# Two gate blocks as a seventeenth pair, k rows written once in a third buffer, and the first output projection ordered by hand

## The chip, the cores and the metric

The kernel runs on one core of a Trainium2 chip. What is measured is device time in microseconds (us), the median of the timed runs. One more execution is recorded by the hardware profiler; every duration of a single instruction comes from that one. The engines are PE (matrix products), DVE (VectorE), ACT (ScalarE), POOL (GpSimd) and SP, which here only issues DMA transfers, all of them in one queue.

## The reference

One encoder block for a sequence of 1024 rows of width 1024, one layer, all in float32. Cut to what the kernel's stages correspond to:

```python
h = rmsnorm(x, norm_w) * (1 + scale) + shift           # scale, shift, gate from c @ w_ada
(a_bg, a_cg, a_x, a_z, q, k, v, z_b, a_raw, b_raw,
 gate_a_raw, gate_b_raw) = split(h @ w_in)
ya = a_cg * dwconv_centred(a_bg * a_x, conv_a_w)        # width 3
ya = (ya * silu(a_z)) @ w_pa
q, k, v = silu(dwconv_centred([q, k, v], conv_qkv_w))   # width 5, 8 heads of 128
q, k = l2norm(q), l2norm(k)
...
for n in chunks:                                        # gated delta rule, forwards and backwards
    v_new = u[n] - w[n] @ S
    o[n] = q_dec[n] @ S + a_qk[n] @ v_new
    S = S * gl[n] + k_dec[n].T @ v_new
...
o = rmsnorm_per_head(o_forward + o_backward) * gdn_norm_w
yb = (o * silu(z_b)) @ w_pb
merged = sigmoid(gate_a_raw) * ya + sigmoid(gate_b_raw) * yb
out = rmsnorm(x + gate * (merged @ w_o), final_norm_w)
```

u and w come from a triangular inverse for each chunk of each head.

## The kernel before

**Blocks.** The sequence lies along the free dimension, and the 1024 features of h are eight tiles of 128 partitions, each split into two parts, hhi and hlo, whose sum is the float32 value. A column block of w_in is 128 outputs wide. Its product is 3 x 8 x 2 = 48 matmuls of 128x512: high weights by hhi, high weights by hlo, low weights by hhi, for eight tiles and two halves of the sequence. A weight block (`wtile`, line 1123) is two DMAs of 256 KB from SP's queue, a rounding copy on ACT (wh) and a subtraction on POOL (wl) for each half. The gate blocks are named ga0 to ga7 (for the first mixer) and gb0 to gb7, their results pass through a sigmoid and are stored to sga_d and sgb_d.

**Heads.** For each head h one column block each of k, q, v and z is computed. Then `prep_k` (line 770) transposes kT to get row norms (ktp), builds the decay matrices D and the gram product, and inverts 32x32 blocks: 30 pairs of steps (et, E) on POOL, with DMAs through memory before and behind. `prep_q` (851) forms q times the decays (the row of decays er is loaded by DMA, 861), transposes kT once more for the rows of k (ktk, copied to ktok, 883) and v for vp. `merge` (906) joins the 32x32 blocks into 128x128 with small matmuls (psy, psu, pst, psz, psv), with copies on DVE and ACT between. `chain` (983) runs eight steps of state product (cb from S and kT), solve (cb from r and N), scaled copy (vw) and update (cb from vw and ktok), both directions at once. Its output lies in vp, is normalized there, and `head_out` (1065) transposes it (otp), multiplies by silu(z) and stores it to yb_d.

These routines are generators. A scheduler records what they yield (line 294) and issues PE's instructions in an order of its own (line 203), from a table of costs; once issued the order is fixed. `fill` (1078) feeds it the column blocks between: k, q, v and z of the heads, and gate blocks, with three (RESERVE, line 26) held to the end; `choose` (1093 to 1097) picks the next. The pair PLAIN = (2, 6) (line 27) says that gb0 and gb1 are among them, that gb2 to gb5 are run as plain blocks behind the heads, and gb6 and gb7 behind the pairs.

**Pairs.** The 32 column blocks of the first mixer (bg, ax, cg, az) run as 16 pairs (`Pair`, 1189): two column blocks by two halves of the sequence and of the features, with seven products of 12 matmuls instead of eight, 84 matmuls a pair. The operands are sums of weights (DVE), a rounding copy (ACT) and a subtraction (POOL); `slots` (1180) gives them places, four in the weight buffers hi and lo and two in buffers of their own. Weights are prepared five products ahead (AHEAD). `mixed` (1279) consumes the results; behind the az pair of blocks j and j+1 the two y are stored to y_d. The first pair and the last one ("last", 1329) have products in an order of their own.

**Gate blocks and first output projection.** Behind the pairs come gb6 and gb7 (`gate_block`, 1332). The eight tiles of y are loaded from y_d and split into yhi and ylo before gb7 (1364 to 1378). Then the projection by w_pa (1392 to 1416): for each block pa0 to pa7 the weights, the gate sga, the weights wadag of the third part of w_ada, 48 matmuls, a product with the gate, the store to m_d, eight small DVE operations that make ga from wadag, `gate_column` (1388) for the block before, and the split of one tile blo of yb. The pool bs has two buffers for sga and one for wadag, and the order of the engines other than PE is the program scheduler's here, while it is written by hand (`manual_schedule`) in the pairs. Behind it come the projection by w_pb (pb) and the last one by w_o (fo).

## Time and profile before

| what | us |
|---|---|
| median of 3 runs (lowest, highest) | 1502.65 (1497.63, 1503.92) |
| the profiled execution, whole | 1494.86 |
| its span, first to last instruction | 1493.1 |

The mean granted clock of PE in that execution is 0.978 of full speed. By stage of the profiled execution, in us from its start, with the time in which PE was busy:

| stage | from, to | PE busy | granted clock |
|---|---|---|---|
| conditioning, norm, first k | 0, 128 | 102.0 of 128 | 0.84 |
| heads, with gate blocks between | 128, 813 | 653.4 of 685 | 0.99 |
| plain gate blocks gb2 to gb5 | 813, 859 | 46.0 of 46 | 0.98 |
| 16 pairs | 859, 1174 | 310.7 of 315 | 1.00 |
| gb6, gb7, first projection (pa) | 1174, 1307 | 118.1 of 133 | 0.95 |
| second projection (pb) | 1307, 1397 | 90.0 of 90 | 1.00 |
| last projection (fo) | 1397, 1493 | 89.6 of 96 | 0.99 |

A row of such a table counts time in which PE had any instruction, so a PE that runs its instructions at a lower clock, or with a start that waits for each, still reads as busy. In rows of single instructions the columns are the start, the duration, the engine, the line of the kernel, and in brackets how long the engine had been idle before it and what it waited for.

### The profile page before, as it was taken

The numbers are of one execution on the slowest core, as the hardware profiler recorded it, in microseconds if no ns is written. First come the engines' busy times: TensorE is split into PE (matmuls) and PEld (weight loads), VectorE is DVE, ScalarE is ACT, GpSimd is POOL, SyncE is SP. The second block draws the span as 40 slices with busy tenths as digits, with TensorE's granted clock in tenths as the row PEclk, the third lists the DMA queues.
The fourth block names the chain that finished last, engine by engine and source line by source line (L and its number), as shares of the span: only waits on it lengthen the run. The fifth ranks groups of instructions, "written<-read, shape, count | busy, mean of one in ns | idle before, by whom it ended". The sixth has DMA issues, their size and how long they took to land.

```text
span 1493.1 us, 22782 instructions
## 1 busy us (share of the span) xinstructions
PE 1409.8 (94%) x8602; PEld 1168.1 (78%) x8602; DVE 843.4 (56%) x1457; ACT 621.2 (42%) x1498; POOL 690.4 (46%) x861
## 2 busy tenths in 40 slices
PE   4899999999999999999997999999999969999998
PEld 3687878787878787878886878787878758888886
DVE  7959227557666667566524736565657364423335
ACT  5227728657574737474533333222232251122211
POOL 6103649553668448654712654544545122255301
PEclk7799999999999999999999999999999989999999
DMA  8213341412423231513221220303030465455502
GB/s 322 93 40 124 98 125 72 114 50 69 118 63 100 58 113 29 142 30 86 69 60 57 99 99 29 113 29 113 29 106 22 158 255 197 156 191 173 193 14 99
DMA packets 123581, 153.37 MB, mean 103 GB/s; under 512 B 74704, under 2 KB 75088, under 8 KB 123472
## 3 DMA queue, kind: packets, MB, share of 16 engines
q1 hardware_dynamic: 123184, 151.14, 31.6%
q8 instruction: 67, 1.10, 0.3%
q10 hardware_dynamic: 288, 0.79, 0.1%
q14 instruction: 42, 0.34, 0.1%
HBM read 122.40 MB, written 29.49 MB: 102 GB/s over the span
## 4 chain that ended last, share of the span: by engine, by line
PE 66%; DVE 12%; POOL 7%; ACT 6%; DMA 5%; issue 4%; SPq 1%; POOLq 0%; ACTq 0%; DVEq 0%
PE pp_ga L203 6%; PE cb L203 4%; PE pp_q L203 4%; PE ps_ax_S L1233 3%; PE pp_k L203 3%; PE ps_bg_S L1233 3%; PE ps_cg_S L1233 3%; PE pp_z L203 3%; PE ps_az_S L1233 2%; POOL E L294 2%; PE o L203 2%; POOL et L294 2%; PE pp_pb L1138 2%; PE pp_pb L1140 2%; PE pp_pb L1139 2%
## 5 line engine op out<-in xcount | busy, mean ns | idle before, releaser
L294 POOL TENSOR_TENSOR E<-E,et 128x30 f32<-128x30 f32 (+7 forms) x240 | 122.3, 509 | 17.3
L294 POOL TENSOR_TENSOR et<-E 128x30 f32<-128x30 f32 (+7 forms) x240 | 113.1, 471 | 26.1 <-DMA E<-s 9.9
L294 ACT ACTIVATE vw<-cb,cols 128x128 f32<-128x128 f32 x112 | 35.8, 365 | 104.0 <-PE cb L203 103.9
L294 ACT ACT_TABLE_LOAD x49 | 62.9, 1283 | 1.5 <-PEq L1570 0.8
L294 DVE SCALAR_TENSOR_TENSOR S<-S,exps,cb 128x128 f32<-128x128 f32 x96 | 29.1, 342 | 60.8 <-PE cb L203 60.7
L1138 PE MATMUL pp_pa<-yhi,wh_pa 128*128 128x512 f32 x128 | 52.3, 408 | 6.9 <-ACT yhi L1375 6.9
L1130 POOL TENSOR_TENSOR wl_pa<-wr_pa,wh_pa 128x512 fp32r<-128x512 f32 x16 | 24.1, 1523 | 72.3 <-ACT wh_pa L1129 72.3
L1140 PE MATMUL pp_pa<-yhi,wl_pa 128*128 128x512 f32 x128 | 51.7, 404 | 3.0 <-POOL wl_pa L1130 3.0
L203 PE MATMUL pp_ga<-hhi,wh_ga 128*128 128x512 f32 x128 | 51.7, 404 | 1.9 <-ACT xpad L294 1.9
L1139 PE MATMUL pp_pa<-ylo,wh_pa 128*128 128x512 f32 x128 | 51.8, 405 | 1.6 <-DVE ylo L1376 1.6
L203 PE MATMUL pp_ga<-hhi,wl_ga 128*128 128x512 f32 x128 | 52.2, 407 | 0.0
L203 PE MATMUL pp_ga<-hlo,wh_ga 128*128 128x512 f32 x128 | 51.7, 404 | 0.0
L203 PE MATMUL pp_z<-hhi,wl_z 128*128 128x512 f32 x128 | 51.4, 401 | 0.0
L203 PE MATMUL pp_z<-hlo,wh_z 128*128 128x512 f32 x128 | 51.2, 400 | 0.0
L203 PE MATMUL pp_z<-hhi,wh_z 128*128 128x512 f32 x128 | 51.1, 399 | 0.0
L1138 PE MATMUL pp_pb<-bhi,wh_pb 128*128 128x512 f32 x128 | 50.6, 395 | 0.0
L1140 PE MATMUL pp_pb<-bhi,wl_pb 128*128 128x512 f32 x128 | 50.5, 395 | 0.0
L1139 PE MATMUL pp_pb<-blo,wh_pb 128*128 128x512 f32 x128 | 50.5, 395 | 0.0
L294 DVE SCALAR_TENSOR_TENSOR kT<-xpad,cvq_t,kT 128x1024 f32<-128x1024 f32 x32 | 47.7, 1490 | 0.3
L294 POOL TENSOR_TENSOR wl_q<-wr_q,wh_q 128x512 fp32r<-128x512 f32 x16 | 20.8, 1304 | 58.2 <-ACT wh_q L294 54.7
L294 DVE SCALAR_TENSOR_TENSOR qT<-xpad,cvq_t,qT 128x1024 f32<-128x1024 f32 x32 | 47.3, 1480 | 0.4
L294 DVE SCALAR_TENSOR_TENSOR N<-gram,cols,D 128x128 f32<-128x128 f32 x128 | 34.6, 342 | 22.1 <-PE gram L203 16.9
(764 smaller groups left out, 4654.4 us busy)
## 6 DMA issues: line engine op xcount, KB each, us to landing
wada<-in_wada SPq DMA_DIRECT2D x16, 512.0 KB, 7.5
D<-gr_d SPq DMA_DIRECT2D x16, 512.0 KB, 7.8
xt<-in_x SPq DMA_DIRECT2D x8, 512.0 KB, 8.9
wr_k<-in_win SPq DMA_DIRECT2D x16, 256.0 KB, 3.1
wr_q<-in_win SPq DMA_DIRECT2D x16, 256.0 KB, 3.2
wr_v<-in_win SPq DMA_DIRECT2D x16, 256.0 KB, 4.3
wr_ga<-in_win SPq DMA_DIRECT2D x16, 256.0 KB, 3.1
qg<-er_d SPq DMA_DIRECT2D x8, 512.0 KB, 6.2
```

The costliest lines, as they stand in the source:

```text
L203: getattr(self.pe, what)(out, *ins, **kw)
L294: self._sched.record(self._name, lambda: real(*args, **kw), outs, ins, cost, extra, table, op == "memset")
L1130: G.tensor_tensor(lo[:, ch(q, 512)], raw, hi[:, ch(q, 512)].bitcast(F32), ALU.subtract)
L1138: PE.matmul(ps, wh, mhi[k][:, sl], start=i == 0, stop=False)
L1139: PE.matmul(ps, wh, mlo[k][:, sl], start=False, stop=False)
L1140: PE.matmul(ps, wl, mhi[k][:, sl], start=False, stop=i == KT - 1)
L1233: PE.matmul(ps, w[:, ch(m)], r, start=first and m == i == 0, stop=m == 3 and i == 2, skip_group_check=True)
```

## The change

**k rows.** `prep_k` now writes ktok from the transposes ktp that it makes anyway, in three buffers instead of two. The second transposition ktk in `prep_q` goes. One of the two rows of decays is loaded into the buffer vp of the head instead of a buffer of its own (er); so vp is taken earlier, and the wait for the output of head h - 2, whose buffer it is, stands ahead of the load.

**Gate blocks.** PLAIN is (0, 4): the heads' fill has ga0 to ga7 alone, the plain blocks behind the heads are gb0 to gb3. gb4 and gb5 become a seventeenth pair (`stored`), which now is the "last" one. gb6 and gb7 stay behind the pairs. `slots` starts at another place of its six, so that the last product of 17 pairs falls on the same one.

**Before the first projection.** At the fourth-last product of the pairs the program takes the buffers of y, both weight blocks gb6 and gb7, and issues the loads of y. Three tiles of y are split ahead of gb6, five ahead of gb7, and pa0's weights stand between.

**The first projection.** Its order is by hand now. sga, wadag and blo of block j + 1 are fetched at the start of block j, wadag has two buffers, and `gate_column(j)` stands behind block j, no longer one later.

Where instructions stand now is shown at three places. The first is PE's queue at the end of head 6's chain. The names are: o6 the output of the chain, pp_z6 and pp_z7 the column blocks z of heads 6 and 7, psy7 and psu7 the small products that join head 7's inverse, otp6 the transposes of head 6's output. Before:

```order
L203 MATMUL pp_z6_1_7607<-hhi6_574,wl_z6_7275 128x512
L203 MATMUL pp_z6_1_7607<-hhi7_621,wh_z6_7274 128x512
L203 MATMUL pp_z6_1_7607<-hlo7_622,wh_z6_7274 128x512
L203 MATMUL pp_z6_1_7607<-hhi7_621,wl_z6_7275 128x512
L203 MATMUL otp6_0_7670<-ident_72,vp6_6803 128x128 x4
L203 MATMUL otp6_1_7678<-ident_72,vp6_6803 128x128 x4
L203 MATMUL pp_z7_0_7685<-hhi0_101,wh_z7_7556 128x512
```

And after the change, where the row o6 is the last product of the chain:

```order
L204 MATMUL o6_0_7084<-vn6_1_7_7484,D1_6_5679 128x128
L204 MATMUL pp_z6_1_7412<-hlo5_534,wh_z6_6934 128x512
L204 MATMUL pp_z6_1_7412<-hlo7_622,wh_z6_6934 128x512
L204 MATMUL pp_z6_1_7412<-hhi7_621,wl_z6_6935 128x512
L204 MATMUL psy7_7550<-T64_7_7082,N0_7_6479 32x32
L204 MATMUL psy7_7550<-y64_7_7083,N0_7_6479 32x32
...
L204 MATMUL psy7_7550<-y64_7_7083,N1_7_6480 32x32
L204 MATMUL otp6_0_7589<-ident_72,vp6_6506 128x128 x4
L204 MATMUL otp6_1_7595<-ident_72,vp6_6506 128x128 x2
L204 MATMUL psu7_7599<-N0_7_6479,Vb7_7008 32x32 x2
L204 MATMUL psu7_7599<-N1_7_6480,Vb7_7008 32x32 x2
```

Before, the last product of chain 6 stood 69 rows ahead of otp6, and most rows between were column products of v7 and z6, with z7 behind otp6. Now the last eight products of z6 and the 32 small products psy7 stand between them, and the rest of the joining (psu7) comes among the transposes.

The second place is PE's queue at the end of head 7, the last one (o7 the output of its chain, otp7 its transposes, gb and ga7 column blocks). Before:

```order
L203 MATMUL o7_0_7974<-vn7_1_7_8256,D1_7_6598 128x128
L203 MATMUL pp_gb1_1_8203<-hlo6_575,wh_gb1_7942 128x512
L203 MATMUL pp_gb1_1_8203<-hhi6_574,wl_gb1_7943 128x512
L203 MATMUL pp_gb1_1_8203<-hhi7_621,wh_gb1_7942 128x512
L203 MATMUL pp_gb1_1_8203<-hlo7_622,wh_gb1_7942 128x512
L203 MATMUL pp_gb1_1_8203<-hhi7_621,wl_gb1_7943 128x512
L203 MATMUL otp7_0_8297<-ident_72,vp7_7560 128x128 x4
L203 MATMUL otp7_1_8302<-ident_72,vp7_7560 128x128 x4
L1138 MATMUL pp_gb2_0_8391<-hhi0_101,wh_gb2_8355 128x512
```

After:

```order
L204 MATMUL o7_1_7710<-vn7_0_7_8001,D0_7_6477 128x128
L204 MATMUL o7_0_7709<-vn7_1_7_8002,D1_7_6478 128x128
L204 MATMUL pp_ga7_0_7996<-hhi2_103,wh_ga7_7814 128x512
L204 MATMUL pp_ga7_0_7996<-hlo2_107,wh_ga7_7814 128x512
...
L204 MATMUL pp_ga7_1_8042<-hlo7_622,wh_ga7_7814 128x512
L204 MATMUL pp_ga7_1_8042<-hhi7_621,wl_ga7_7815 128x512
L204 MATMUL otp7_0_8083<-ident_72,vp7_7011 128x128 x4
L204 MATMUL otp7_1_8088<-ident_72,vp7_7011 128x128 x4
L1134 MATMUL pp_gb0_0_8177<-hhi0_101,wh_gb0_8141 128x512
```

Five column products of gb1 stood between the last o7 and otp7; now 42 of ga7 stand there, and the first plain block behind is gb0 instead of gb2.

The third place is the queue of SP around the last stores of y (a6, a7) and the loads behind them (wr_ raw weights, ylo the loads of y, sgb_d and sga the gates' stores and loads). Before:

```order
L1316 DMA y_d_87<-a6_10724 128x1024
L1128 DMA wr_gb7_0_11027<-in_win 128x512
L1128 DMA wr_gb7_1_11031<-in_win 128x512
L1370 DMA ylo0_11017<-y_d_87 128x1024
...
L1370 DMA ylo7_11024<-y_d_87 128x1024
L1400 DMA wadag1_11292<-in_wadag 128x1024
L1337 DMA sgb_d_88<-xpad0_116 128x1024
L1128 DMA wr_pa0_0_11098<-in_wpa 128x512
L1128 DMA wr_pa0_1_11102<-in_wpa 128x512
L1398 DMA blo0_11190<-yb_d_89 128x1024
```

After:

```order
L1312 DMA y_d_87<-a6_10510 128x1024
L1124 DMA wr_gb6_0_10893<-in_win 128x512
L1124 DMA wr_gb6_1_10897<-in_win 128x512
L1124 DMA wr_gb7_0_10903<-in_win 128x512
L1124 DMA wr_gb7_1_10907<-in_win 128x512
L1381 DMA ylo0_10883<-y_d_87 128x1024
...
L1381 DMA ylo7_10890<-y_d_87 128x1024
L1337 DMA sgb_d_88<-gb5_10935 128x1024
L1413 DMA sga0_11134<-sga_d_86 128x1024
L1351 DMA sgb_d_88<-xpad0_116 128x1024
L1124 DMA wr_pa0_0_11034<-in_wpa 128x512
L1124 DMA wr_pa0_1_11038<-in_wpa 128x512
L1416 DMA blo0_11120<-yb_d_89 128x1024
```

The weights of both blocks gb6 and gb7 now stand ahead of the loads of y, the weights pa0 behind the gates' stores as before, and one blo stands behind them where all eight stood.

The diff, with unchanged lines left out:

```diff
@@ -24,7 +24,8 @@
 RESERVE = 3
-PLAIN = (2, 6)
+PLAIN = (0, 4)
+LAST = 6
 AHEAD = 5
@@ -772,6 +773,7 @@
         kT = tiles["k", h]
+        ktok = yield big("ktok", f"ktok{h}", 3)
         kss = yield tile_of(gp, [P, 5, NC], "kss", f"kss{h}", 3)
@@ -786,6 +788,7 @@
                 yield tr(ps[:, ch(cc)], kT[:, ch(4 * half + cc)])
+            S.activation(ktok[:, ch(half, 512)], ps, AF.Copy)
             for cc in range(4):
@@ -844,7 +847,7 @@
         Q.dma_start(Vb, s2[1].rearrange("c b r k -> (b r) c k"))
-        ghead[h] = dict(kT=kT, A=D, D=D, N=N, N3=N3, Vb=Vb, bk=bk, wk=wk, sk=kss[:, 3])
+        ghead[h] = dict(kT=kT, ktok=ktok, A=D, D=D, N=N, N3=N3, Vb=Vb, bk=bk, wk=wk, sk=kss[:, 3])
         yield ("mark", ("pk", h))
@@ -858,7 +861,10 @@
         qg = [(yield big("qg0", f"qg0_{h}", 2)), qT]
-        er = [qg[0], (yield big("er", f"er{h}", 1))]
+        if h >= 2:
+            yield ("need", ("out", h - 2))
+        vp = gh["vp"] = yield big("vp", f"vp{h}", 2)
+        er = [qg[0], vp]
         for d in range(2):
@@ -880,18 +886,8 @@
             V.tensor_tensor(qg[d], qT, er[d], ALU.mult)
-        ktok = yield big("ktok", f"ktok{h}", 2)
-        for half in range(2):
-            ps = yield get(pg, f"ktk{h}_{half}", kT)
-            for cc in range(4):
-                yield tr(ps[:, ch(cc)], kT[:, ch(4 * half + cc)])
-            S.activation(ktok[:, ch(half, 512)], ps, AF.Copy)
-            yield free(ps)
-        gh.update(qg=qg, qss=qss, ktok=ktok)
+        gh.update(qg=qg, qss=qss)
         yield ("need", ("v", h))
-        if h >= 2:
-            yield ("need", ("out", h - 2))
-        vp = gh["vp"] = yield big("vp", f"vp{h}", 2)
         vT, sk = tiles["v", h], gh["sk"]
@@ -1175,14 +1171,14 @@
-    place, spare = [2], []
+    place, spare = [-7 * (17 + (LAST - PLAIN[1] - 2) // 2) % 6], []
...
             return [bw.tile([P, 512], F32R, tag=p, name=f"w{p}{name}", bufs=2) for p in "hl"]
-        if i % 2 == 0:
+        if i % 2 == 0 or not spare:
             spare[:] = [wp.tile([P, KT * P], F32R, tag=f"w{p}", name=f"w{p}{name}") for p in ("hi", "lo")]
@@ -1325,8 +1321,26 @@
+    def stored(name, j0, dst, func, place):
+        parts = {}
+
+        def consume(b, half, ps, add):
+            if b not in parts:
+                parts[b] = [bt.tile([P, T], F32, tag="out", name=f"{name}{j0 + b}", bufs=4), 0]
+            o = parts[b][0][:, ch(half, 512)]
+            if add is not None:
+                V.tensor_tensor(o, ps, add, ALU.add)
+                ps = o
+            S.activation(o, ps, func)
+            parts[b][1] += 1
+            if parts[b][1] == 2:
+                Q.dma_start(dst[j0 + b], parts[b][0])
+
+        return Pair(name, j0, consume, place)
+
     pairs = [(n, j) for j in range(0, 8, 2) for n in ("bg", "ax", "cg", "az")]
-    pairs = [mixed(n, j, {0: "first", len(pairs) - 1: "last"}.get(i)) for i, (n, j) in enumerate(pairs)]
+    pairs = [mixed(n, j, None if i else "first") for i, (n, j) in enumerate(pairs)]
+    pairs += [stored("gb", j, sgb_d, AF.Sigmoid, "last" if j + 2 == LAST else None) for j in range(PLAIN[1], LAST, 2)]
     steps = [(p, n) for p in pairs for n in p.order]
@@ -1360,21 +1374,23 @@
             yp = ctx.enter_context(tc.tile_pool(name="yp", bufs=1, reuse_waits="tile", side="right"))
-            ws = [wtile(win[G_B + PLAIN[1]], f"gb{PLAIN[1]}")]
-    yhi = [yp.tile([P, T], F32R, name=f"yhi{k}") for k in range(KT)]
-    ylo = [yp.tile([P, T], F32R, name=f"ylo{k}") for k in range(KT)]
-    for j in range(PLAIN[1], 8):
-        if j < 7:
-            ws.append(wtile(win[G_B + j + 1], f"gb{j + 1}"))
+            yhi = [yp.tile([P, T], F32R, name=f"yhi{k}") for k in range(KT)]
+            ylo = [yp.tile([P, T], F32R, name=f"ylo{k}") for k in range(KT)]
+            ws = [wtile(win[G_B + j], f"gb{j}") for j in (6, 7)]
             for k in range(KT):
                 Q.dma_start(ylo[k].bitcast(F32), y_d[k])
-        else:
-            wpas = [wtile(wpa[0], "pa0")]
-        if j == 7:
-            for k in range(KT):
-                S.activation(yhi[k], ylo[k].bitcast(F32), AF.Copy)
-                V.tensor_tensor(ylo[k], ylo[k].bitcast(F32), yhi[k].bitcast(F32), ALU.subtract)
-        gate_block(j, ws.pop(0))
+
+    def split(hi, lo):
+        S.activation(hi, lo.bitcast(F32), AF.Copy)
+        V.tensor_tensor(lo, lo.bitcast(F32), hi.bitcast(F32), ALU.subtract)
+
+    for k in range(3):
+        split(yhi[k], ylo[k])
+    gate_block(6, ws[0])
+    wpas = [wtile(wpa[0], "pa0")]
+    for k in range(3, KT):
+        split(yhi[k], ylo[k])
+    gate_block(7, ws[1])
     sctx.close()
@@ -1389,31 +1405,35 @@
-    with tc.tile_pool(name="bs", bufs=2, reuse_waits="tile") as bs:
+    with tc.tile_pool(name="bs", bufs=2, reuse_waits="tile") as bs, tc.manual_schedule(engines=others):
+        sgs, wts = [], []
+
+        def fetch(j):
+            sgs.append(bs.tile([P, T], F32, tag="sg", name=f"sga{j}"))
+            Q.dma_start(sgs[j], sga_d[j])
+            wts.append(bs.tile([P, KT, P], F32, tag="wadag", name=f"wadag{j}"))
+            Q.dma_start(wts[j], wadag[j])
+            Q.dma_start(blo[j].bitcast(F32), yb_d[j])
+
+        fetch(0)
         for j in range(8):
-            with tc.high_priority():
-                if j < 7:
-                    wpas.append(wtile(wpa[j + 1], f"pa{j + 1}"))
-                w = wpas.pop(0)
-            Q.dma_start(blo[j].bitcast(F32), yb_d[j])
-            wt = bs.tile([P, KT, P], F32, tag="wadag", name=f"wadag{j}", bufs=1)
-            Q.dma_start(wt, wadag[j])
-            sg = bs.tile([P, T], F32, tag="sg", name=f"sga{j}")
-            Q.dma_start(sg, sga_d[j])
+            if j < 7:
+                wpas.append(wtile(wpa[j + 1], f"pa{j + 1}"))
+                fetch(j + 1)
+            sg, wt = sgs[j], wts[j]
             for half in range(2):
-                ps = product(w, yhi, ylo, half, f"pa{j}")
+                ps = product(wpas[j], yhi, ylo, half, f"pa{j}")
                 V.tensor_tensor(sg[:, ch(half, 512)], ps, sg[:, ch(half, 512)], ALU.mult)
-            Q.dma_start(m_d[j], sg)
-            ga = bs.tile([P, P], F32, tag="ga", name=f"ga{j}")
-            V.tensor_scalar(ga, wt[:, 0, :], sc_t[:, 0:1], None, ALU.mult)
-            for d in range(1, KT):
-                V.scalar_tensor_tensor(ga, wt[:, d, :], sc_t[:, d : d + 1], ga, ALU.mult, ALU.add)
-            gsum.append(ga)
-            if j:
-                gate_column(j - 1)
-            S.activation(bhi[j], blo[j].bitcast(F32), AF.Copy)
-            V.tensor_tensor(blo[j], blo[j].bitcast(F32), bhi[j].bitcast(F32), ALU.subtract)
-        gate_column(7)
+                if half:
+                    Q.dma_start(m_d[j], sg)
+                    continue
+                ga = bs.tile([P, P], F32, tag="ga", name=f"ga{j}")
+                V.tensor_scalar(ga, wt[:, 0, :], sc_t[:, 0:1], None, ALU.mult)
+                for d in range(1, KT):
+                    V.scalar_tensor_tensor(ga, wt[:, d, :], sc_t[:, d : d + 1], ga, ALU.mult, ALU.add)
+                gsum.append(ga)
+                split(bhi[j], blo[j])
+            gate_column(j)
...
     fp = ctx.enter_context(tc.tile_pool(name="fp", bufs=1, reuse_waits="tile", side="right"))
```

## The prediction

> **What bounds the kernel now.** I read the page's totals first, then the busy times by stage, then what TensorE (PE) waited for, then the two places with the longest waits row by row.
>
> ```profile
> span 1493.1 us, 22782 instructions
> PE 1409.8 (94%) x8602; PEld 1168.1 (78%) x8602; DVE 843.4 (56%) x1457; ACT 621.2 (42%) x1498; POOL 690.4 (46%) x861
> ...
> core 0: us, PE busy (x) PEld busy (x) DVE busy (x) ACT busy (x) POOL busy (x), PEclk, DMA share, GB/s
> 600.00:700.00 100.00, 94.19 (x957) 80.15 (x955) 58.65 (x130) 55.43 (x163) 51.92 (x89) 1.00 0.35 93
> 760.00:813.00 53.00, 44.94 (x324) 39.20 (x324) 15.08 (x45) 19.47 (x61) 9.00 (x6) 0.96 0.15 51
> 858.00:1174.00 316.00, 311.71 (x1347) 251.72 (x1346) 182.02 (x208) 90.27 (x155) 153.25 (x113) 1.00 0.20 69
> 1174.00:1215.00 41.00, 30.07 (x115) 22.94 (x114) 19.83 (x33) 15.54 (x21) 5.08 (x4) 0.88 0.80 305
> 1215.00:1240.00 25.00, 21.80 (x88) 16.93 (x87) 14.32 (x15) 10.43 (x14) 8.91 (x5) 0.93 0.31 110
> ```
>
> PE is busy 94% of the span, next comes VectorE (DVE) with 56%. The stages say where the rest is: a stretch of heads loses 6 of 100 us, the pairs (858 to 1174) lose 4 of 316, but the end of the heads loses 8 of 53, and the two stretches after the pairs 14 of 66, with the granted clock down to 0.88. So PE's own work sets the time, plus two holes.
>
> ```profile
> PE otp L203 <- DVE vp L294: 8.1, 1, 8.1
> PE pp_pa L1138 <- ACT yhi L1375: 6.9, 1, 6.9
> PE pp_pa L1140 <- POOL wl_pa L1130: 3.0, 1, 3.0
> PE pp_gb L1138 <- ACT wh_gb L1129: 2.0, 1, 2.0
> ```
>
> The holes have names: the last head's transposes wait 8.1 us for its normalized output, and the gate blocks and first output projection wait for y, for its split and for weights.
>
> **PE's own work.** The change takes the 64 transposes ktk out (kT was transposed a second time for them), moves two blocks of 48 wide matmuls out of the heads, and adds a pair of 84 for them.
>
> ```profile
> 577.60 1.09 PE L203 MATMUL ktp<-ident,kT 128*128 128x128 f32 x8 [0.99 <-ACT kT L294]
> 1174.63 0.40 PE L1138 MATMUL pp_gb<-hhi,wh_gb 128*128 128x512 f32 x1
> 1185.56 0.40 PE L1140 MATMUL pp_gb<-hhi,wl_gb 128*128 128x512 f32 x1
> ```
>
> The last two rows are the first and last of one block's 48 matmuls: 10.93 us over 47 steps, 0.2326 us each. Two blocks cost 96 x 0.2326 = 22.3, a pair 84 x 0.2326 = 19.5. Eight transposes end after 1.09, the last of them taking about 0.27 by itself, so one step is (1.09 - 0.27)/7 = 0.117, and 64 make 7.5. Sum: -22.3 - 7.5 + 19.5 = **-10.3**. The 16 copies to ktok on ScalarE (ACT) stay, only earlier; ACT is 42% busy and they hide there. If that cover went, they would cost 16 x 0.6 = 10 at most. The pair brings four loads, as the two blocks did, and seven splits of 1.3 on POOL instead of four; POOL is busy 153 of 316 us in that stage, and 9 more in 19.5 fit the same share. Which weights share a buffer shifts too: the second and third product of the first pair now wait for gb3 to end before their split can start (ACT 0.6 and POOL 1.3 each, beside a first product of 2.8); I take 0, with 2 as its upper bound.
>
> **The end of the heads.**
>
> ```profile
> 801.93 0.38 PE L203 MATMUL o<-vn,D 128*128 128x128 f32 x2
> 811.54 1.94 PE L203 MATMUL otp<-ident,vp 128*128 128x128 f32 x8 [8.06 <-DVE vp L294]
> 814.13 0.63 PE L1140 MATMUL pp_gb<-hhi,wl_gb 128*128 128x512 f32 x1
> ```
>
> From the last chain product to the transposes of its output pass 9.6 us (sums of squares on ACT, a power on GpSimd (POOL), scaling on DVE). Before, five gate matmuls stand in that gap; now 42 of ga7 do, 42 x 0.2326 = 9.8. The wait of 8.1 goes, and with it the slow restart behind it (transposes 1.94 for 1.09, matmuls of 0.63 for 0.40): 2 more. **-10.** What is late next is nothing: gb0 follows at once.
>
> Head 6 gets the opposite. Its chain's last product is now followed by 8 z6 matmuls (1.9 us) and the small products psy7, and then its own transposes otp6, since z7 is held back until they are issued and ga6 and ga7 stand behind z7.
>
> ```profile
> 662.92 0.21 PE L203 MATMUL psy<-T,N 32*32 32x32 f32 x1
> ...
> 664.06 0.50 PE L203 MATMUL pp_z<-hlo,wh_z 128*128 128x512 f32 x1
> ...
> 667.13 0.23 PE L203 MATMUL psu<-N,Vb 32*32 32x32 f32 x4 [1.18 <-DVE Vb L294]
> ...
> 672.63 1.15 PE L203 MATMUL psz<-T,N 64*64 64x64 f32 x32 [2.19 <-DVE T L294]
> ```
>
> psy takes 1.1. So otp6 waits 9.6 - 1.9 - 1.1 = 6.6, and 1.5 for a slow restart: **+8**. Bounds: nothing, if psy itself is held so that otp6 is ready behind it (the wait then stands one row earlier, rival 2), and 10 with a full slow window. The same rows price the merge of head 6, which loses its fill: from psy to psz PE lost 1.2 + 2.2 = 3.4 with 16 z5 matmuls (3.7) between; now 4 transposes and 2 matmuls (0.9) stand there, so 3.4 + 3.7 - 0.9 = 6.2 are lost: **+3**, between 0 and 6.
>
> Chain 0 loses ga6 as its fill: its steps 5 to 7 have only 8 transposes beside them.
>
> ```profile
> 474.86 0.61 PE L203 MATMUL cb<-vw,ktok 128*128 128x128 f32 x4
> 476.22 0.61 PE L203 MATMUL cb<-S,kT 128*128 128x128 f32 x4
> 477.54 0.61 PE L203 MATMUL cb<-r,N 128*128 128x128 f32 x4
> 478.24 0.62 ACT L294 ACTIVATE vw<-cb,cols 128x128 f32<-128x128 f32 x2
> ```
>
> Bare latency of a step: 1.4 from state product to the next, 1.3 to the solve, 0.7 to the scaled copy, and about 0.4 back, an estimate of 3.5 where the two directions overlap. Its 10 products are 20 instructions of 0.112, 2.2 us. So 1.2 stay empty in step 6, about 1.3 in step 7, 0.5 in step 5: **+3**; zero if the copies of other heads happened to stretch the steps anyway, 6 if each step takes 4.5.
>
> **Gate blocks and first projection.**
>
> ```profile
> 1307.15 0.48 PE L1138 MATMUL pp_pb<-bhi,wh_pb 128*128 128x512 f32 x1
> 1176.32 6.81 SPq L1316 DMA_DIRECT2D y_d<-a  x2
> 1184.49 5.25 SPq L1370 DMA_DIRECT2D ylo<-y_d  x8
> 1193.86 3.16 SPq L1128 DMA_DIRECT2D wr_pa<-in_wpa  x2
> 1204.97 1.22 ACT L1129 ACTIVATE wh_pa<-wr_pa 128x512 fp32r<-128x512 f32 x2 [14.01 <-DMA wr_pa<-in_wpa]
> ```
>
> From the first gate matmul (1174.63) to the second projection (1307.15) pass 132.5; ten blocks need 10 x 48 x 0.2326 = 111.6, the eight column products about 2. So 19 are lost. The rows show the chain: the stores of the last y come 2 and 8 us after the last pair, gb7's weights, the loads of y and pa0's weights queue behind them, and ACT splits y only behind pa0's weights. Now the y pair is followed by 19.5 us of gate pair, the loads of y may start after its fourth product, 3 x 12 x 0.2326 = 8.4 before it ends, and 22.3 us of two plain blocks come before y is needed. Loads issued over 5 us that land within 11 to 16 fit. pa0's weights can be issued when gb6 is done, 11.2 before use; they took 11.1 (1193.86 to 1204.97) behind the eight loads of y. Those now start some 17 us earlier, seen from the blocks, so I take 4 to 6. In the projection one blo load at a time replaces eight, and the gate column's sums (eight small DVE operations a block) and the split of blo fit into a block's 11.2 us of matmuls; if they did not, each block would wait for its psum bank. I take **-18** and leave 1; bounds -19, and -9 if half of it returns.
>
> ```profile
> L1130 POOL TENSOR_TENSOR wl_pa<-wr_pa,wh_pa x16: 1271/1296/4017, 1205.7 to 1285.6; 128x512 fp32r<-128x512 f32 x16
> ...
> 1222.91 6.24 POOL L1130 TENSOR_TENSOR wl_pa<-wr_pa,wh_pa 128x512 fp32r<-128x512 f32 x2 [14.69 <-ACT wh_pa L1129]
> ...
> 1220.05 5.75 DVE L1415 TENSOR_TENSOR blo<-blo,bhi 128x1024 fp32r<-128x1024 f32 x5
> ```
>
> Two of POOL's subtractions take 6.2 beside five of DVE's splits, 2.6 otherwise. Five splits of y now stand beside pa0's, so 3.7 of my 4 us of slack there may go. The Trainium skill, "SBUF — State Buffer", section "Who interferes with whom", says that a DVE instruction with two SBUF inputs contends with a GpSimd one that reads SBUF, and that the loser blocks for the whole instruction. By that rule, with all five splits winning, the sum would be some 5 us worse; the rows show the two taking turns, so I stay with the row.
>
> **Sum:** -10.3 - 10 - 18 + 8 + 3 + 3 = **-24**. The profiled execution took 1494.86 (span 1493.1 and 1.8 around it), so 1470.5 by its own measure. The three timed runs have their median at 1502.65, 0.5% above it; what is measured is such a median, so I predict **1478**.
>
> **Rivals.** (1) The heads lose no new time: another fill happens to cover otp6, the merge and chain 0. For it speaks that small shifts decide; against it, that the order is fixed and PE cannot pass a waiting instruction. -24 - 14 = -38: 1465.
>
> (2) The inverse on POOL becomes the bound at the merges.
>
> ```profile
> L294 POOL TENSOR_TENSOR E<-E,et 128x30 f32<-128x30 f32 (+7 forms) x240 | 122.3, 509 | 17.3
> L294 POOL TENSOR_TENSOR et<-E 128x30 f32<-128x30 f32 (+7 forms) x240 | 113.1, 471 | 26.1 <-DMA E<-s 9.9
> 523.03 1.16 PE L203 MATMUL gram<-kT 128*128 128x128 f32 x8 [1.11 <-ACT N L294]
> 539.23 0.13 POOL L294 MEMSET E<- 64x16 f32 x1 [14.93 <-DMA E<-s]
> 591.96 0.23 POOL L294 TENSOR_TENSOR E<-E,et 128x15 f32<-128x15 f32 x1
> 602.44 0.21 PE L203 MATMUL psy<-T,N 32*32 32x32 f32 x1
> ```
>
> Head 5 needs 16 from gram to the first step, 53 for the steps, 10 to psy: 79. Bare steps are 235.4/8 = 29.4 per head, so 55 is the least. In the new order 61 us of PE work stand between gram7 and psy7, with 70 to 87 in the heads before. I count nothing; if head 7 takes 79 like head 5, PE stands 15 to 18 there: 1495.
>
> (3) The transition keeps half its loss, by transfers of y that still delay pa0's weights or by POOL as above: 1486.
>
> (4) Slower than before: the load queue in the heads. The row of decays (er) now lands in the v buffer and waits until the transposes of two heads ago have read it; the next weights are queued behind it on SyncE. In the order, at least 25 us of PE work stand between those transposes and the first use of those weights, more than twice the 11.1 that even pa0's load took behind the eight of y.
>
> Only if six heads each stalled over 5.3 us (32 in all) would the result pass 1510; at 8 each it is 1478 + 48 = 1526.
>
> **How the numbers follow.** Forecast 0.50, (1) 0.20, (2) 0.15, (3) 0.10, (4) 0.05. The range takes in (1) to (3) and the bounds: 1461 to 1496. Within 0.5% (7.5 us, about what a measurement can tell) lies only the upper edge of (2) and (3): faster 0.87, same 0.08, slower 0.05.
>
> **What would show it.** Right: PE's wait for vp at otp7 gone and one of 5 to 7 us at otp6; waits before pp_gb and pp_pa under 2 in all; granted clock near 1 through the transition; gb0 starting near 785 and the second projection near 1284. Wrong: psy waiting for Vb or N after DMA (rival 2), pp_pa on wl_pa or yhi (3), wh_q, wh_z or wh_k on DMA in the heads (4).

## The result, and the profile after

The changed kernel took 1487.71 us in the median of six runs (1486.81 to 1488.79), beside 1498.45 for the kernel before on the same chip (1495.45 to 1503.92): a ratio of 0.9922, with a 95% interval from 0.9902 to 0.9942. That is 10.7 us less, where the prediction said 24. The profiled spans are 1485.2 and 1493.1, so 7.9 less. The time lies within the stated range, at less than half of the forecast gain. Of the experiments below, one run of the kernel with the old rows of k took 7528 us, five times as long as any other, and its median leaves that run out.

From the page of the changed kernel, and its view of what PE waited for (total in us, times, longest):

```profile
span 1485.2 us, 22649 instructions
PE 1402.8 (94%) x8526; PEld 1161.1 (78%) x8526; DVE 858.9 (58%) x1466; ACT 614.0 (41%) x1495; POOL 691.8 (47%) x864
...
PE psz L204 <- ACT T L295: 7.3, 3, 5.6
PE psy L204 <- DVE N L295: 5.2, 1, 5.2
PE cb L204 <- ACT vn L295: 3.9, 3, 1.7
PE psy L204 <- DVE T L295: 3.5, 1, 3.5
...
PE ps_gb_S L1229 <- DVE gb L1332: 2.8, 1, 2.8
```

PE's busy time fell by only 7, to the same share of 94%. The two holes that the prediction named, otp7 (8.1) and yhi (6.9), are gone from the list. In their place stand waits before psy, psu, pst and psz, the small products that join the inverse of a head (13.3 of them in head 6), and one of 2.8 in the last pair.

The same stages of both kernels, by windows (busy times of PE, its weight loads, DVE, ACT and POOL, then granted clock, DMA share, GB/s). Of the kernel before, from the first product of ga0 to the first plain block, and from the last y pair (az6) to the second projection:

```profile
127.84:813.13 685.29, 653.66 (x5320) 555.71 (x5321) 399.65 (x832) 392.36 (x1094) 375.59 (x610) 0.99 0.29 81
1154.38:1307.15 152.77, 137.22 (x581) 110.18 (x580) 75.73 (x119) 38.49 (x55) 36.91 (x27) 0.96 0.53 188
```

Of the changed kernel the same two, then its last pair alone and the merge of head 6:

```profile
127.19:798.71 671.52, 632.08 (x5161) 537.37 (x5161) 397.86 (x835) 378.08 (x1081) 367.58 (x606) 0.97 0.28 79
1138.60:1298.89 160.29, 154.28 (x666) 123.75 (x664) 87.44 (x127) 45.85 (x67) 43.05 (x33) 0.99 0.55 189
1157.84:1183.93 26.09, 21.90 (x86) 16.87 (x85) 10.76 (x13) 10.16 (x16) 8.94 (x7) 0.93 0.56 207
660.00:700.00 40.00, 26.67 (x340) 22.41 (x339) 25.94 (x50) 20.65 (x54) 16.83 (x34) 0.79 0.48 120
```

The heads shrank by 13.8 (685.3 to 671.5), though 29.8 of PE work left them: PE is idle 39.4 there instead of 31.6, and the granted clock fell from 0.99 to 0.97. Behind them the stretch grew by 7.5 with 19.5 of pair in it, a gain of 12 where 18 was forecast. The last pair takes 26.1, and around head 6's merge PE is idle 13.3 of 40 us at a clock of 0.79.

The merge of head 6 in the timeline of the changed kernel: two rows of PE, then DVE, then ACT, then the first and the last step of the inverse on POOL.

```profile
672.72 0.25 PE L204 MATMUL psy<-T,N 32*32 32x32 f32 x1 [5.19 <-DVE N L295]
...
685.33 1.97 PE L204 MATMUL psz<-T,N 64*64 64x64 f32 x32 [5.61 <-ACT T L295]
...
665.28 0.43 DVE L295 STREAM_TRANSPOSE T<-N 32x256 f32<-32x256 f32 x1 [7.31 <-DMA N<-s]
...
668.19 1.78 DVE L295 STREAM_TRANSPOSE N<-Vb 32x256 f32<-32x256 f32 x4 [0.41 <-DMA Vb<-s]
669.99 3.71 DVE L295 SCALAR_TENSOR_TENSOR N<-gram,cols,D 128x128 f32<-128x128 f32 x14
...
679.19 4.92 DVE L295 SCALAR_TENSOR_TENSOR qT<-xpad,cvq_t,qT 128x1024 f32<-128x1024 f32 x3
684.02 0.40 DVE L295 COPY N<-psu 32x256 f32<-32x256 f32 x1
...
684.46 0.37 ACT L295 ACTIVATE N<-psu 32x256 f32<-32x256 f32 x1 [4.28 <-DVE N L295]
...
601.77 0.24 POOL L295 TENSOR_TENSOR et<-E 128x30 f32<-128x30 f32 x1 [1.11 <-DMA E<-s]
...
656.89 0.24 POOL L295 TENSOR_TENSOR E<-E,et 128x15 f32<-128x15 f32 x1
```

The inverse came late: from the first product of gram6 (578.9) to psy passed 94 us, with 80 of PE work between them. From there one engine after another stood still. DVE waits 7.3 for the block that returns from memory, with head 7's gram products behind it in its queue. Its transposes for psy end at 669.97; PE starts psy at 672.72. What held it for the last 2.7 the rows don't say for certain; it may be that psy takes a result buffer of the pool that gram7 had filled, and that DVE empties only now. The last two products of q7 stand behind psy on PE, so q7's convolution on DVE (qT) begins late, and that one stands ahead of DVE's copy N from psu, for which ACT waits 4.3 and PE, at psz, 5.6.

Head 7's merge waits too, for another reason. PE, then DVE:

```profile
735.93 0.24 PE L204 MATMUL psy<-T,N 32*32 32x32 f32 x2 [3.51 <-DVE T L295]
...
734.72 0.17 DVE L295 SCALAR_TENSOR_TENSOR oss<-oss,qss 128x8 f32<-128x8 f32 x1 [6.71 <-ACT sqj L295]
...
735.45 0.89 DVE L295 STREAM_TRANSPOSE T<-N 32x256 f32<-32x256 f32 x2
```

The transposes of head 7 (T from N) stand on DVE behind a tiny operation on head 6's output (oss), which waits 6.7 for ACT's squares. So the 6 us of waiting that were forecast at otp6 are there (3.5, 0.7, 1.1 and 0.4 make 5.7), but all except the last 0.4 at psy7.

The last pair: ACT, PE, and the queue of SP. A11 and S4 are two of its seven products (the rows ps_gb_A with wloA, and the rows ps_gb_S with whS behind the wait), and e1 is ACT's copy of the result of A11.

```profile
1174.40 0.63 ACT L1125 ACTIVATE wh_gb<-wr_gb 128x512 fp32r<-128x512 f32 x1 [3.43 <-DMA wr_gb<-in_win]
...
1176.49 0.58 ACT L1236 ACTIVATE e_gb<-ps_gb_A 128x512 f32<-128x512 f32 x1
...
1173.37 0.39 PE L1229 MATMUL ps_gb_A<-hhi,wloA_gb 128*128 128x512 f32 x1
...
1179.33 0.50 PE L1229 MATMUL ps_gb_S<-hhi,whS_gb 128*128 128x512 f32 x1 [2.81 <-DVE gb L1332]
...
1180.51 0.63 PE L1229 MATMUL ps_gb_S<-hlo,whS_gb 128*128 128x512 f32 x1
...
1161.95 4.02 SPq L1312 DMA_DIRECT2D y_d<-a  x2
1166.01 7.32 SPq L1124 DMA_DIRECT2D wr_gb<-in_win  x4
```

A11 is done by 1173.8, but ACT copies it (e1) only at 1176.49: ahead of it stand the copies of gb7's weights, which wait for transfers that SP could issue only behind the stores of y. PE waits 2.8 for what follows e1, and from 0.8 us behind the wait a matmul takes 0.63 instead of 0.39, for some 3 us. The blocks from there to the second projection take 115.0 (1183.93 to 1298.89), against a forecast of 114.6 (111.6 of blocks, 2 of columns, 1 left).

### The profile page after: what moved, and what is told of

Its sections match the earlier page's. It is cut to its first block, busy times and chain, and to the rows that moved or that the text cites. A ratio compares the mean times of both kernels' runs of the same rounds, so it can differ in the third digit from the quotient of the medians.

```text
span 1485.2 us, 22649 instructions
## 1 busy us (share of the span) xinstructions
PE 1402.8 (94%) x8526; PEld 1161.1 (78%) x8526; DVE 858.9 (58%) x1466; ACT 614.0 (41%) x1495; POOL 691.8 (47%) x864
## 4 chain that ended last, share of the span: by engine, by line
PE 67%; DVE 12%; POOL 8%; ACT 5%; DMA 4%; issue 2%; SPq 1%; POOLq 0%; ACTq 0%; DVEq 0%
PE pp_ga L204 6%; PE cb L204 4%; PE pp_q L204 4%; PE pp_k L204 4%; PE ps_ax_S L1229 4%; PE ps_cg_S L1229 3%; POOL E L295 3%; POOL et L295 3%; PE o L204 3%; PE ps_bg_S L1229 3%; PE ps_az_S L1229 2%; PE pp_pb L1134 2%; PE pp_pb L1135 2%; PE pp_pb L1136 2%; PE fo L1501 2%
## 5 line engine op out<-in xcount | busy, mean ns | idle before, releaser
L1126 POOL TENSOR_TENSOR wl_pa<-wr_pa,wh_pa 128x512 fp32r<-128x512 f32 x16 | 20.4, 1295 | 86.6 <-ACT wh_pa L1125 86.6
L295 ACT ACT_TABLE_LOAD x42 | 53.9, 1283 | 1.4 <-PEq L1590 0.8
L295 POOL TENSOR_TENSOR wl_ga<-wr_ga,wh_ga 128x512 fp32r<-128x512 f32 x16 | 23.2, 1455 | 65.9 <-ACT wh_ga L295 65.8
L204 PE MATMUL pp_q<-hhi,wl_q 128*128 128x512 f32 x112 | 46.7, 417 | 2.1 <-POOL wl_q L295 2.1
L295 DVE SCALAR_TENSOR_TENSOR r<-cb,negeg,vp 128x128 f32<-128x128 f32 x112 | 34.0, 344 | 23.7 <-PE cb L204 23.4
L295 DVE SCALAR_TENSOR_TENSOR qT<-xpad,cvq_t,qT 128x1024 f32<-128x1024 f32 x32 | 47.2, 1474 | 0.5
```

Of the source, the lines that this page charges most:

```text
L204: getattr(self.pe, what)(out, *ins, **kw)
L295: self._sched.record(self._name, lambda: real(*args, **kw), outs, ins, cost, extra, table, op == "memset")
L1126: G.tensor_tensor(lo[:, ch(q, 512)], raw, hi[:, ch(q, 512)].bitcast(F32), ALU.subtract)
```

## The experiments

Ratios are to the kernel before, in runs on the same chip. "Heads" is the stretch from the first product of ga0 to the first plain block in the profiled execution, and "lost" what is left of it when the bare steps of PE's instructions there are taken off: 646.5 us of work before, 617.0 in the changed kernel, 624.3 with eight gate blocks and the old rows of k, 639.3 with ten and the new ones.

| kernel | us | ratio (95%) | heads | lost |
|---|---|---|---|---|
| before | 1498.45 | | 685.3 | 38.8 |
| changed | 1487.71 | 0.9922 (0.9902, 0.9942) | 671.5 | 54.5 |
| k rows as before | 1481.29 | 0.9905 (0.9869, 0.9940) | 667.6 | 43.3 |
| pair undone, ten blocks in heads | 1488.09 | 0.9932 (0.9909, 0.9955) | 682.2 | 42.9 |
| projection as before | 1484.05 | 0.9913 (0.9883, 0.9943) | 672.4 | 55.4 |
| ten blocks, gb6 and gb7 as pair | 1479.76 | 0.9883 (0.9850, 0.9917) | 687.3 | 48.0 |
| low weights on DVE | 1485.57 | 0.9909 (0.9879, 0.9939) | 676.5 | 59.5 |
| tail: columns and gb7's weights later | 1483.38 | 0.9910 (0.9878, 0.9943) | 673.2 | 56.2 |
| planner: POOL 15% dearer | 1468.50 | 0.9801 (0.9776, 0.9826) | 652.3 | 35.3 |
| planner: POOL 20% dearer | 1490.45 | 0.9949 (0.9931, 0.9967) | 675.9 | 58.9 |
| ten blocks and pair, POOL 20% dearer | 1468.68 | 0.9810 (0.9784, 0.9837) | 675.9 | 36.6 |
| kernel before, POOL 15% dearer | 1509.25 | 1.0067 (1.0051, 1.0084) | 700.4 | 53.9 |
| POOL 15% dearer, tail mended | 1461.29 | 0.9756 (0.9730, 0.9783) | 656.3 | 39.3 |
| POOL 5% dearer, tail mended | 1478.08 | 0.9870 (0.9846, 0.9894) | 671.6 | 54.6 |

**One part undone at a time.** Theory A: the heads lack column products to stand beside their chains. Theory C: the inverse of head 6 comes late whatever PE does. Theory B is the prediction's sum. The label POOL 15% dearer and its like mean that the scheduler's table of costs was changed; "tail mended" names the edits behind the heads, shown last. First the rows of k as before:

```diff
 (prep_k)
-            S.activation(ktok[:, ch(half, 512)], ps, AF.Copy)
 (prep_q)
+        for half in range(2):
+            ps = yield get(pg, f"ktk{h}_{half}", kT)
+            for cc in range(4):
+                yield tr(ps[:, ch(cc)], kT[:, ch(4 * half + cc)])
```

> The changed kernel, with the rows of k made as before (64 second transposes ktk, two buffers, a buffer of its own for er). PE has 7.5 us more work in the heads than the changed kernel. Theory A (the heads are short of column products: the stalls at the merge of head 6, at psy7 and in chain 0 come from too little work between dependent steps): in PE's order 73 us of work then stand between gram6 and psy6 where 80 stood, but 3.6 and 3.3 us beside the merge of head 6 instead of 1.9 and 1.5, and 13.7 us between the last o6 and otp6 instead of 3.1. So the waits at psz6 (5.6) and psy7 (3.5) go to under 2 each, and the sum comes out level or faster: 1480 to 1488 us. Theory B (the sum of the prediction: the transposes cost their work, the stalls are where they are for other reasons): 7.5 slower, 1495. Theory C (the inverse of head 6 on POOL is late, whatever PE does): psy6 still waits 4 to 6 us, 1492 to 1497.

Its window of the heads and its longest wait before psy:

```profile
127.07:794.63 667.56, 640.17 (x5225) 543.81 (x5225) 398.22 (x832) 381.14 (x1081) 376.91 (x606) 0.98 0.28 79
...
PE psy L204 <- ACT vp L295: 4.6, 2, 2.6
```

Theory B is out: with 7.5 us more work the kernel is no slower, and its heads are 4.0 shorter, about as much as two executions of one order differ (below). psy waits at most 2.6. This speaks for A, and taking out the 64 transposes gained nothing that could be told in the heads of the changed kernel.

```diff
-PLAIN = (0, 4)
-LAST = 6
+PLAIN = (2, 6)      # and az6 "last"; y loaded and split around gb6 as before
```

> The changed kernel with ten gate blocks in the heads, four plain ones behind, 16 pairs (az6 the last), gb6 and gb7 behind them with the loads and splits of y where they were before; rows of k and the first projection as changed. PE has 22.3 - 19.5 = 2.8 us more work than the changed kernel. Theory A (the heads are short of column products): with the two blocks back the merge of head 6, psy7 and chain 0 lose some 25 us less than in the changed kernel, and otp7 has 11.1 us of work ahead of it, so the first plain block begins 17 to 20 earlier than that of the kernel before (near 795); behind the pairs some 8 of the before's 10 us of waits for y return. 1475 to 1482 in all. Theory C (POOL's inverse is late, whatever PE does): psy6 or psy7 still waits 5 or more, and the first plain block begins near 805: 1488 to 1495.

```profile
126.74:808.91 682.17, 650.52 (x5257) 551.69 (x5257) 412.29 (x840) 389.04 (x1093) 373.35 (x610) 0.98 0.29 81
...
PE psy L204 <- DVE N L295: 8.2, 1, 8.2
```

The first plain block began at 808.9, later than either theory had it and nearer C's 805, and the total is that of the changed kernel, at the edge of C's range. psy still waits 8.2, in head 6, with ten blocks in the heads: against A, for C. And with ten blocks and the new rows of k the first plain block began 4 us earlier than before, not 17, though the wait at otp7 is gone here as well.

```diff
-        fetch(0) ... fetch(j + 1) ... gate_column(j)
+        (the loop of the kernel before, in the scheduler's order)
```

> The changed kernel with the first output projection as before (order by the program's scheduler, one buffer for wadag, loads of yb at once, column of the gate one block later). If the order by hand carries part of the gain behind the pairs (eight loads of yb ahead of the weights of pa1 and pa2, and POOL's subtractions beside the splits): 4 to 7 slower than the changed kernel, 1492 to 1495, with a wait before pp_pa of 3 or more and a clock below 0.95 there. If the gain comes from the early y alone: within 2 us of the changed kernel, and faster by the 3 us that the eight column products now wait (psg, 0.4 each and the gap behind): 1485.

1484.05: within the noise of the changed kernel, as the second case has it. With y early, the order by hand of the first projection carried no gain that could be told. With y late it may carry some: from the first product of gb6 to the second projection pass 132.5 us before, 126.7 in the kernel with the pair undone, which has the order by hand and still waits for y (4.4 and 2.9), and 115.0 with y early in the changed kernel.

So each of the three parts, undone alone, leaves the total where the changed kernel has it (ratios 0.9905, 0.9932 and 0.9913 for 0.9922): no single part carries the 10.7 us.

```diff
-PLAIN = (0, 4)
-LAST = 6
+PLAIN = (2, 6)
+LAST = 8            # no plain block behind the pairs; all of y split at once
```

> The changed kernel with ten gate blocks in the heads (gb0, gb1 again), gb2 to gb5 plain, and gb6 and gb7 as the seventeenth pair, with no plain block behind it; PE's work is the same as in the changed kernel. Theory A (the heads are short of column products): the heads lose some 25 us less; behind the pairs y has only the pair's 19.5 us to be stored, loaded and split, and the projection waits 3 to 8 for the last splits: 1465 to 1472. Theory C (POOL's inverse is late, whatever PE does): the heads gain 5 to 10 at most, 1482 to 1490. If y needs more than the pair by 15 or more, 1480 under theory A too, and the wait then stands before pp_pa.

```profile
126.39:813.64 687.25, 651.48 (x5256) 551.96 (x5257) 413.91 (x840) 388.71 (x1093) 372.78 (x610) 0.98 0.29 81
...
PE psy L204 <- DVE N L295: 8.5, 1, 8.5
```

1479.76 lies between the two ranges, 2 below C's: psy waits 8.5, again in head 6, and the heads lose 6.5 less than in the changed kernel, both as C has it; the waits for y's splits before pp_pa are 3.7, as A has it. The order of the heads is that of the kernel with the pair undone, and yet they took 687.3 instead of 682.2: two executions of one order differ by 5 us there.

**Is POOL too slow?** The low parts of the heads' weights are subtracted on DVE:

```diff
-LW = "gg"
+LW = "vv"
```

> The changed kernel with the low parts of the weights in the heads subtracted on DVE instead of POOL; the planner orders the rest anew. If the inverse is late because POOL has 10 to 17 us of other work in its midst (17.4 of 55.4 in head 6): its stretch falls to 40 to 46 in every head, the wait at psy6 goes, 1476 to 1483. If it is late because POOL's steps stand still while DVE works on two operands of SBUF (steps of 0.24 alone and 1.25 beside DVE's wide multiply-adds): the steps of a head grow from 26 to 33 to over 33, and the total stays or grows, 1487 to 1495.

```profile
123.30:799.81 676.51, 632.83 (x5160) 540.34 (x5161) 418.92 (x901) 381.55 (x1083) 283.94 (x537) 0.96 0.29 79
...
PE psy L204 <- DVE N L295: 8.1, 2, 6.3
```

POOL's stretch for an inverse fell from 41 to 55 us to 33 to 45, further than the first case has it, though in two heads the steps themselves grew to 38, as the second has it. The heads did not get shorter, psy waits 8.1 in two heads, and 1485.57 lies between the two cases. A shorter stretch on POOL was not enough here. Since DVE got the work that POOL lost, and the order changed too, the run doesn't say which of these took the gain back.

**The order alone.** The cost that the planner (the scheduler of the heads) holds for POOL's elementwise operations was raised; the work stays the same:

```diff
-            return (0.31 + 1.95 * n if "tensor" in op ...
+            return (0.356 + 2.243 * n if "tensor" in op ...
```

> The changed kernel; only the cost that the planner of the heads holds for POOL's elementwise operations is raised by 15%, so the same work is issued in another order (79 to 93 us of PE work between gram and psy of heads 2 to 7, where 60 to 80 stood; the merge of head 6 has 2.8 and 4.4 us beside it). Theory C (the order is planned for an inverse that is faster than it is on the chip, and engines stand behind the merge): the waits at psy together go from 12.5 us to below 4, and what PE loses from 660 to 700 from 18.7 to below 7; otp7 has only 2.3 of work ahead and waits some 7, and chain 0 loses 3 more: 1478 to 1483. Theory A (eight gate blocks are too little work for the heads, wherever they stand): the losses move but their sum stays, the first plain block begins within 3 us of 799, 1485 to 1490.

```profile
127.65:779.94 652.29, 627.74 (x5161) 535.47 (x5161) 393.94 (x830) 362.86 (x1066) 375.67 (x606) 0.99 0.30 82
...
PE otp L204 <- DVE vp L295: 7.4, 2, 7.1
...
PE psy L204 <- DVE N L295: 1.3, 1, 1.3
```

1468.50, 19 us less than the changed kernel with the same matrix products in another order, and 10 below theory C's range. (ACT loads its function tables, 1.28 us each, 28 times in the heads instead of 38; but with 20% it does so 32 times, and the kernel before with 15% 33 times instead of 45, and neither is fast.) psy's longest wait is 1.3; otp7 waits 7.1 again. So what the forecast missed in the heads was a loss of the order. That the order was wrong because it was planned for too fast an inverse, as theory C has it, the next runs don't bear out.

> The changed kernel with POOL's elementwise operations 20% dearer for the planner instead of 15%. Work is the same; 82 to 97 us of PE work stand between gram and psy of heads 2 to 7, but only 5 beside chain 0 (11.9 at 15%), 16.4 beside chain 7, 6.4 ahead of otp6 and 0.2 ahead of otp7. If the gain of the 15% is one of waits at the merges taken away, not of one lucky order: no wait at psy or psz over 3 us in the heads 2 to 7, chain 0 loses 5 more than at 15% and otp7 and chain 7 some 4 more: 1472 to 1480. If it was a lucky order: 1484 to 1492, with waits at psy as in the changed kernel.

```profile
125.11:801.04 675.93, 636.07 (x5161) 537.73 (x5161) 404.30 (x835) 369.36 (x1075) 374.94 (x606) 0.98 0.29 79
...
PE otp L204 <- DVE vp L295: 14.4, 6, 9.4
PE psz L204 <- ACT T L295: 10.5, 6, 3.0
```

Here both cases are half wrong. No wait at psy is over 1.0, so the waits at the merges did go; but psz adds up to 10.5 over six heads, otp waits 14.4 and chain 0 has little beside it, and the total, 1490.45, lies in the range of a lucky order. That a wait goes does not mean that its time is saved.

> The kernel before the change, with POOL's elementwise operations 15% dearer for the planner of the heads; the work is the same. If the 19 us that the same edit brought the changed kernel came from taking away its waits at the merges and behind them: the kernel before has few of these (its waits at psy are 0.2 us, at psz 6.5), so there is little to gain, and its new order has only 8.6 us of work beside chain 7 where 19 stood and still nothing ahead of otp7: 1493 to 1505. If the dearer POOL makes any order of the heads better: 1478 to 1484.

1509.25, slower than the kernel before and 4 above the first case's range. The dearer POOL is no general gain.

> As the kernel with POOL 15% dearer for the planner and the three edits behind the heads, but POOL only 5% dearer. Work is the same. In PE's order 73 to 82 us stand between gram and psy of heads 2 to 6, 62 in head 7; 2.4 and 3.2 beside the merge of head 6, 5.2 ahead of otp6, 9.7 ahead of otp7, 15.3 beside chain 0. From the first product of ga0 to the first plain block PE has 617 us of work; the changed kernel loses 54.5 there, 35.3 with 15%, 58.9 with 20%. If the loss follows what stands beside each wait (theory C, place by place): merge 6 loses 4 to 5 instead of 14.3, merge 7 3 to 6 as its inverse has little time, chain 0 2 to 4 more than with filler, otp7 nothing: 38 to 44 lost, 1463 to 1470. If the order of the heads is a matter of scatter that these sums don't foretell: 45 to 60 lost, 1470 to 1486.

```profile
127.00:798.55 671.55, 639.28 (x5160) 542.29 (x5161) 395.73 (x828) 378.05 (x1077) 376.15 (x606) 0.97 0.28 79
...
PE psy L204 <- ACT y L295: 7.0, 4, 6.5
```

The merge of head 6 no longer waits, as the order promised, but psy7 waits 6.5, and the merges of heads 2 to 5 wait 4 more: 54.6 lost in all, the same as in the changed kernel. The second case holds.

```diff
 # tenpair with gate_column(j - 1) and POOL 20% dearer
```

> Ten gate blocks in the heads, gb6 and gb7 as the seventeenth pair with no plain block behind it, the gate's column one block later, and POOL's elementwise operations 20% dearer in the planner. PE's work is that of the changed kernel. In PE's order 70 to 97 us stand between gram and psy of every head, 7.2 between o6 and otp6, 11.6 between o7 and otp7. Theory C: the waits at psy fall below 4 (8.5 before psy6 with ten blocks and the old plan), the first plain block begins near 797 instead of 813, and the total is 1460 to 1466. Theory A (with ten blocks the heads are full and PE's own work bounds them): no change from ten blocks in the old plan but for the columns, 1476 to 1480.

Its first plain block began at 802.6, not 797, psy waits 5.9 in head 7, not below 4, and 1468.68 is between the two cases. Ten blocks in the heads lost 36.6 in this order, against 48.0 in that of the kernel with ten blocks and the pair.

**Behind the heads.** gb7's weights and y are asked for one product later, and the columns stand one block later:

```diff
-            ws = [wtile(win[G_B + j], f"gb{j}") for j in (6, 7)]
+            ws = [wtile(win[G_B + 6], "gb6")]
+        if i + 3 == len(steps):
+            ws.append(wtile(win[G_B + 7], "gb7"))      # and the loads of y
...
-            gate_column(j)
+            if j:
+                gate_column(j - 1)
```

> The changed kernel with two edits behind the heads: the weights of gb7 and the loads of y are requested one product later (behind A11 of the last pair instead of ahead of it), and the column product of each block of the first projection stands one block later, as before the change. If the last pair's wait (2.8 us at S4) comes from ACT, which holds the copy e1 behind the copies of gb7's weights that wait for their transfer (e1 at 1176.5, 3 us after A11 ended): the pair takes 21 to 22 instead of 26.1, and the eight columns lose 0.25 each instead of 0.5: 5 to 7 us faster than the changed kernel, 1480 to 1483. Rival: gb7's weights or y are then late themselves: waits of 1 to 3 before pp_gb or pp_pa take it back, 1486 to 1488.

The window of the last pair, ACT's copy e1, and PE in pa0:

```profile
1159.59:1180.99 21.40, 20.02 (x86) 15.77 (x85) 10.09 (x13) 8.35 (x13) 6.39 (x5) 1.00 0.27 97
...
1175.54 0.60 ACT L1236 ACTIVATE e_gb<-ps_gb_A 128x512 f32<-128x512 f32 x1 [2.78 <-PE ps_gb_A L1229]
...
1211.89 0.50 PE L1135 MATMUL pp_pa<-ylo,wh_pa 128*128 128x512 f32 x1 [1.27 <-DVE ylo L1387]
```

The cause of most of the last pair's loss is shown: e1 no longer waits for weights, and the pair takes 21.4, 4.7 less. Some 1.5 of these are the slow matmuls: four kernels with the old place of gb7's weights (old rows of k, low weights on DVE, POOL 15% and 20% dearer) had the wait of 2.8 to 3.2 without slow matmuls behind it, and their last pair took 24.5 to 24.9. But y came late in its turn: pa0 waited for its splits, 1.3 the longest time, and took 14.8, where each block behind it takes 11.1, and of the stretch from az6 to the second projection only 3.7 were gained (160.3 to 156.6). With y ahead of gb7's weights, on top of the order with 15%:

> The changed kernel with POOL 15% dearer for the planner, and behind the heads: the loads of y directly behind gb6's weights, gb7's weights one product later (behind A11 of the last pair), the gate's column one block later. Before, the later request of both gb7's weights and y freed the last pair (26.1 to 21.4) but made y late: pa0 14.9 instead of 11.1. With y ahead of gb7's weights both should hold: the pair 21 to 22, pa0 11.2, columns 0.25 each: 5 to 7 us less than with the dearer POOL alone, 1461 to 1464. Rival: the eight transfers of y delay gb7's weights, a wait of 2 to 4 before pp_gb: 1465 to 1468.

```profile
129.71:786.04 656.33, 630.40 (x5160) 538.45 (x5161) 395.83 (x830) 363.00 (x1066) 374.33 (x606) 0.98 0.29 81
1127.37:1280.27 152.90, 150.46 (x666) 123.35 (x664) 86.41 (x128) 45.95 (x67) 44.51 (x34) 1.00 0.57 198
1146.61:1168.02 21.41, 20.02 (x86) 15.77 (x85) 10.10 (x13) 8.35 (x13) 6.39 (x5) 1.00 0.65 240
```

The three stretches are the heads, from az6 to the second projection, and the last pair. From az6 on it takes 152.9, 7.4 less than in the changed kernel: 4.7 in the pair, and 2.7 in the blocks behind it (112.3 for 115.0), whose columns now stand a block later. The whole took 1461.29 us, in the forecast range: 2.4% less than the kernel before, and by the two ratios some 1.7% less than the changed one.

## Why the prediction was right and where it was wrong

- **PE's own work, -10.3.** Right. Counted by bare steps the heads lost 29.5 us of work, forecast 29.8, and the pair came on top.
- **otp7, -10.** Right: no wait there is left, and none came directly behind it.
- **otp6, +8.** Near in size (5.7 of waits and a slow restart), but 5.3 of it at psy7, the bound that the text gave as "psy itself is held"; what held it was DVE's queue, which stood at head 6's output, and not a late inverse.
- **Chain 0, +3.** Right: the waits before cb in chain 0 rose from 0.7 to 4.6.
- **The merge of head 6, +3, "between 0 and 6".** This step failed. It priced the merge by the latencies of one in which the inverse had come in time (3.4 of waits) and asked only for the fill. In the changed kernel the inverse was late, and the waits were 13.3 (5.2, 0.3, 2.2 and 5.6), so 10 more instead of 3. The prediction had this mechanism as its second rival, at 15 to 18 us, but in head 7 and behind 61 us of PE work; head 6 was counted as safe. There POOL needed 55.4 us from the first step to the last (601.8 to 657.1), 12.8 of them for other work and 5.7 idle ahead of it, waiting for weights (18.5 together, where an expectation above has 17.4); before it needed 42.8, with 7.2 of other work and next to no such idle time. The steps themselves grew only from 31.6 to 33.2.
- **The transition, -18.** Half right: -12. Early y did what it should: no wait for y or for pa0's weights, and the blocks took 115.0 where 114.6 were forecast. The term that failed is the pair's, 19.5 by its bare steps: it took 26.1, mostly because the copies of gb7's weights stand ahead of e1 on ACT. With those moved it takes 21.4.
- **What the sum left out.** With 10 in place of 3 for the merge the forecast for the heads would have been -18.8 (-29.8 - 10 + 8 + 10 + 3); it was -13.8. A part of the other 5 is work that ran slower: from 671.6 to 688.7, in the merge of head 6, the granted clock is 0.50 and PE is busy for 7.9 us, which at full clock would take about half (an estimate from these two figures); the term for the merge had no slow restart in it. Of the 15.7 us that the heads lost more than before (54.5 for 38.8), 7.8 are idle time of PE and the rest is PE running slower than its bare steps. Two executions of one order differ by 5 us as well, so the sum is not split further.
- **The level.** The prediction set out from a median of three runs, 1502.65; that of six is 1498.45. From there -24 would have been 1474, so that 1478 lies as near to 1487.71 as it does is in part luck. The signs in time were missed: gb0 began at 798.7, not 785, and the second projection at 1298.9, not 1284.

The first rival, heads that lose nothing new, is out; the third, a transition that keeps a part of its loss, came true by another path than the text gave, and its 1486 is near the measured time by luck, as two thirds of the miss lie in the heads. Of the fourth, weights that come late in the heads, PE shows only 2.1 us of waits (for wl_q). In the order of the changed kernel about half of the PE work taken from the heads came back as lost time; in that with POOL 15% dearer nothing did. What stays open is which property makes one order good. Five kernels with the same eight blocks and new rows of k (the changed one, POOL 5%, 15% and 20% dearer, low weights on DVE) lost between 35 and 60 us in the heads; the amount of work beside each wait foretold where PE would wait, but not the sum.

## What to carry to other kernels

Where every engine's queue is written out beforehand, as here, work that is taken from one engine can be worth less than its time when the other queues no longer fit: look, behind each place where filler leaves, for the instruction of another engine that stands ahead of the one that is waited for. Before such a change is judged, the same work should be run in two or three other orders; here they differed by 22 us, twice what the change itself brought. And a load that is asked for earlier has a copy that waits for it on an engine: put that copy behind what the running products need from that engine.
